# The written order of an attention stage, with another table of prices for changes of work on TensorE

## The chip, the cores and the metric

The kernel runs on one core of one Trainium2 chip. The metric is the device time of one execution in microseconds (us). The kernel before took 1474.77 us (median of three runs, 1473.16 to 1475.11).

## The reference, cut to what matters

One layer of a decoder is computed for a prompt of 1024 tokens and, beside it, for 8 sequences of 8 new tokens each with 2048 cached ones (64 rows, "the sample"). The change is in the order of the attention, which has no softmax. For each of 8 heads of 64 channels:

```
z = q k^T / 8 + bias(head)
log_1mb = log_sigmoid(-z) where key < query, else 0
after   = cumsum(log_1mb) over the keys, from the last key back, without the key itself
a       = exp(log_sigmoid(z) + after) where key < query, else 0
out     = a v
```

The prompt attends to its own 1024 keys; the sample attends to its 8 new keys and to 2048 cached ones, which are gathered page by page (128 keys) through a page table. Around it stand an input projection, a convolution group, an output projection, layer norms and a gated feed-forward part; the change leaves all of these alone.

## The kernel before, in words

The kernel runs stage after stage: the modulation and input projection, the attention stage, the output projection and layer norm with the first block of the up-projection, the up-projection, and the down-projection. In the trace of before the attention stage's first product starts on TensorE at 320.9 us from the start of the span, and the output projection has TensorE to itself from 618.2 us on.

The prompt's part of the attention is 96 steps, each one block of 126 keys against up to 256 queries of a pair of heads. A step's chain of work runs through all engines: `qk` (scores, TensorE, L1044 and L1045, and on blocks at the diagonal a mask product, L1048), `exp` and `ln` (ScalarE), `soft_c` (VectorE, L1055), `hi` (VectorE, L1083: the rounded half of a split) and `lo` (GpSimd, L1086: the rest), `tri` (TensorE, L1090: the running sum over keys as a product with a triangle of -1, once with each half), `weigh` (ScalarE: exp) and `accumulate` (TensorE, L1100: weights times values, two heads in two halves of the array's columns). Scores stand in 4 PSUM buffers, and the ScalarE output in 6 SBUF buffers.

The sample's part is 32 steps, each two pages of two sequences: `pages` (a load of four times 512 KB), `s_scores` (TensorE, L1233, in quarters of 32 columns of the array), `s_bias` (ScalarE), `s_turn` (TensorE, L1242: a transpose), `s_exp`, `s_ln` (ScalarE), `s_soft` and `s_after` (VectorE, L1055 and L1262), `s_tri` (TensorE, L1272 and L1273), `s_weigh` (ScalarE) and `s_values` (TensorE, L1289, in quarters of 32 columns). The pages have 6 buffers, three steps' worth.

So TensorE does four kinds of work here, which the texts below call by these letters:

- r: float32r products on the whole array (`qk`, `tri`);
- f: float32 products on the whole array (`s_turn`, `s_tri`, and small ones: `rms_b` L1117, `s_out` L1301, `last_values` L999);
- h: float32 on halves of the array's columns (`accumulate`);
- q: float32 on quarters of the columns (`s_scores`, `s_values`).

A float32 product stands in the trace as two MATMUL records, a float32r product as one. "Behind" is used for what TensorE does next: TensorE runs its list in order.

Nothing is ordered by hand. `attention_plan` writes down every piece of work with an engine, a cost in us, a priority (in prompt steps: `h` plus an offset for the prompt's work of step h, `at(s) = sb + s*sr` plus an offset for the sample's work of step s) and the work that it depends on. `run_plan` then plays this through: whenever an engine comes free it takes, of the work that could start first, the one with the lowest priority number; a penalty is added on TensorE where the work is of another kind than the last. What comes out is a list, and the kernel issues its instructions on all engines in exactly this order (manual schedule), while semaphores keep the data right. The numbers in `PAR` (offsets, step length, penalty) were found by a search that makes the planned time short. In the kernel before the plan knows three kinds (`TILED`: whole, halves, quarters): a change to the whole array costs 0.1 us (`m0`), one to halves or quarters 0.15 us (`m1`), a change between r and f nothing, and each change adds 3 steps (`md`) to the priority.

Eight blocks of the output projection's weights are loaded at the end of the stage through three staging buffers (`w_load`, SyncE's queue), rounded on VectorE (`w_hi`, L1211) and split on GpSimd (`w_lo`, L1214); their priority is `wo` plus the block's number. The output projection (L1349, L1479) waits for them. Its own order comes from the same `run_plan`, without the penalties and prices that are changed here.

Of the kernel before, what the change touches and what calls it, by code (L numbers as in the profile page):

```python
# [34 lines left out]
HI = "VVVVVVVV"  # L35
LO = "GGGGGGGG"
# [19 lines left out]
SV = ""  # L56
# [79 lines left out]
class Buf:  # L136
# [11 lines left out]
    def free(self, eng):  # L148
# [3 lines left out]
INF = 1e9  # L152
NSTEP = 32
NU = NPG // 2
PAR = dict(sb=10.07, sr=2.613, win=0, page=5.83, qk=-5.975, soft=-4.175, sc=-1.312, ca=-5.853, hi=-6.283,
           lo=-4.398, tri=-2.966, we=-1.97, ac=2.462, ss=-1.798, bi=3.89, tu=-2.19, ab=0.329, sp=-2.015,
           st=1.44, sw=-4.026, sv=2.858, rms=9.705, qp=-6.748, kp=-4.753, wo=85.118, ld=2, le=2, qd=2, qb=2,
           cn=1, cd=1, m0=0.1, m1=0.15, md=3)
LOW = "G" * 8


def attention_plan(par):
# [3 lines left out]
    P = par  # L166

    def add(eng, cost, prio, name, args=(), deps=(), **kw):
        W.append(Work(eng, cost, prio, name, args, deps, **kw))
        return W[-1]  # L170
# [6 lines left out]
    at = lambda s: P["sb"] + s * P["sr"]  # L177
# [24 lines left out]
    blocks = [add("DVE", 0.45, -2, "block_queries", (i,), new[0:1]) for i in range(4)]  # L202

    QK, S3, SC, CA, HI, LO, TRI, WE, AC, OUT, RG = ({} for _ in range(11))
    fre, rg, rcs = [], [], []
    for h, t in enumerate(steps):
        k = 2 * (QC - t.c0)
        z = ("z", h % 4)
        if t.first and t.j:
            prev = max(i for i in range(h) if steps[i].x == t.x)  # L210
        if t.b == max(s.b for s in steps if (s.x, s.j) == (t.x, t.j)) and t.j:
# [6 lines left out]
                 banks=(z,))  # L218
# [4 lines left out]
                    [SC[h], CA.get(h - 2), TRI.get(h - 2), HI.get(h - 1)])  # L223
        eng, cost = ("DVE", 0.068 + 0.00104 * k) if h < P["ld"] or h >= N - P["le"] else ("Pool", 0.1 + 0.0022 * k)
        LO[h] = add(eng, cost, h + P["lo"], "lo", (h,), [HI[h]])
        TRI[h] = add("PE", 0.04 + 0.00083 * k, h + P["tri"], "tri", (h,), [LO[h], HI[h]], banks=(z,))
        WE[h] = add("Activation", 0.054 + 0.00083 * k, h + P["we"], "weigh", (h,), [TRI[h]], banks=(z,))
        if t.b:

# [5 lines left out]
                    banks=(acc,))  # L235
        if t.last and t.j == 7:
            add("DVE", 0.35, h + P["rms"], "out_last", (h,), [AC[h]], banks=(acc,))
        elif t.last:
            n = len(rg)
            OUT[h] = add("DVE", 0.73, h + P["rms"], "out", (h,), [AC[h]] + ([rg[n - 2]] if n >= 2 else []), banks=(acc,))  # L240
            a = add("Activation", 0.31, h + P["rms"], "rms_a", (h,), [OUT[h]] + ([rg[n - 1]] if n else []))
            b = add("PE", 0.45, h + P["rms"], "rms_b", (h,), [a], take="sz")
            c = add("Activation", 0.36, h + P["rms"], "rms_c", (h,), [b], give=b)
# [3 lines left out]
        if t.x == 1 and h // 2 % 12 == 0 and t.p < 3:  # L247
# [8 lines left out]
            r = [d]  # L256
# [3 lines left out]
            for e in range(2):  # L260
                a = add("DVE", 0.6, pr, "k_hi", (p, e), [d])
# [4 lines left out]
            if p == 3:  # L266
                lv = add("DVE", 0.3, pr, "last_load", (), VN[3])
                for i in range(5):
                    a = add("PE", 0.25, pr, "last_values", (i,), [lv], take="sz")
                    b = add("Activation", 0.3, pr, "last_copy", (i,), [a], give=a)  # L270
# [10 lines left out]
    sn = nb  # L281
# [11 lines left out]
    PG, SS, BI, TU, A3, SP, LA, ST, SW, SV, OB, OT = ({} for _ in range(12))  # L293
    for s in range(NSTEP):
        PG[s] = add("DMA", P["page"], at(s) - 9, "pages", (s,), [SV.get(s - 3), PG.get(s - 1)])
        b = (("scr", s % 2),)
        SS[s] = add("PE", 0.86, at(s) + P["ss"], "s_scores", (s,), [PG[s], BI.get(s - 2), ST.get(s - 2), sn, SS.get(s - 1)] + blocks, banks=b)
        BI[s] = add("Activation", 0.36, at(s) + P["bi"], "s_bias", (s,), [SS[s], TU.get(s - 2)], banks=b)
        TU[s] = add("PE", 0.15, at(s) + P["tu"], "s_turn", (s,), [BI[s], SW.get(s - 2), nbv], banks=b, take=s % 2)
        a = add("Activation", 0.265, at(s) + P["ab"], "s_exp", (s,), [TU[s], SP.get(s - 2)], banks=b)  # L300
        A3[s] = add("Activation", 0.31, at(s) + P["ab"], "s_ln", (s,), [a])
        SP[s] = add("DVE", 0.335, at(s) + P["sp"], "s_soft", (s,), [A3[s], ST.get(s - 2), LA.get(s - 1)], banks=b)
        LA[s] = add("DVE", 0.7, at(s) + P["sp"], "s_after", (s,), [SP[s], LA.get(s - 1)])
        ST[s] = add("PE", 0.68, at(s) + P["st"], "s_tri", (s,), [SP[s], LA[s], TU[s]], banks=b)
        SW[s] = add("Activation", 0.265, at(s) + P["sw"], "s_weigh", (s,), [ST[s], SV.get(s - 2)], banks=b, give=TU[s])
        SV[s] = add("PE", 0.88 + (0.5 if s % NU == 0 else 0), at(s) + P["sv"], "s_values", (s,),
                    [SW[s], SV.get(s - 1), OB.get(s - 1), nbv, nbe, zero], banks=(("acc", 1),))
        if s % NU == NU - 1:
            OB[s] = add("DVE", 0.61, at(s) + P["sv"], "s_ob", (s,), [SV[s], OT.get(s - NU)], banks=(("acc", 1),))
            a = add("PE", 0.43, at(s) + P["sv"] + 1, "s_out", (s,), [OB[s]], banks=(("acc", 0),))  # L310
            OT[s] = add("DVE", 0.7, at(s) + P["sv"] + 1, "s_osT", (s,), [a], banks=(("acc", 0),))
    e = at(NSTEP) + 2
    a = add("Activation", 0.27, e, "o_a", (), [OT[NSTEP - 1]] + rg[-2:])
# [31 lines left out]
    return 2.2 if a == "DMA" else 0.28 if b == "PE" else 0.15 if (a, b) == ("Activation", "DVE") else 0.2  # L345


TILED = {"s_scores": 32, "s_values": 32, "accumulate": 64}
PORT = {"hi", "q_hi", "k_hi", "k_copy", "fix_zero", "block_queries", "rms_gain", "o_gain", "w_hi"}
HOLD = {"lo", "q_lo", "k_lo", "w_lo", "q_ones"}  # L350

# [1 line left out]
def run_plan(W, P):  # L353


    lat, win, tune = 0.2, P["win"], "sb" in P
    mode, held = [128], {"DVE": [0.0, 0.0], "Pool": [0.0, 0.0]}

    def switch(w):
        m = TILED.get(w.name, 128)  # L360
        return 0.0 if not tune or w.eng != "PE" or m == mode[0] else P["m0"] if m == 128 else P["m1"]

    def keeps(w):
        return tune and (w.eng == "DVE" and (w.name in PORT or w.name in HOLD) or w.eng == "Pool" and w.name in HOLD)
    free, bank, region, out, rings = {}, {}, {0: 0.0, 1: 0.0}, [], {k: list(v) for k, v in P.get("rings", {}).items()}
    succ, need = {}, {}
    for w in W:
        need[w] = len(w.deps)
        for d in w.deps:
            succ.setdefault(d, []).append(w)  # L370
    ready = {}
    for w in W:
        if not need[w]:
            ready.setdefault(w.eng, []).append([0.0, w])

    def start(r, w):
        s = max(r, free.get(w.eng, 0.0))
        for b in w.banks:
            e, t = bank.get(b, (None, 0.0))
            if e != w.eng:  # L380
                s = max(s, t + lat)
        if keeps(w):
            a, b = held["Pool" if w.eng == "DVE" else "DVE"]
            if a <= s < b:
                s = b
        if w.take == "sz":
            t = min(region.values())
            s = max(s, t)
        elif w.take is not None:
            s = max(s, region[w.take])  # L390
        new = {}
        for b in w.uses:
            if b.slot is None:
                l = rings.setdefault(b.ring, [])
                i = len(l) + new.get(b.ring, 0)
                new[b.ring] = new.get(b.ring, 0) + 1
                if b.before and b.before.slot is None:
                    s = INF
                if i >= b.n:
                    s = max(s, l[i - b.n].free(w.eng))  # L400
        return s

    while True:
        best = None
        for e, l in ready.items():
            if not l:
                continue
            c = [(start(r, w), w) for r, w in l]
            m = min(s for s, _ in c)
            if m >= INF:  # L410
                continue
            s, w = min(((s, w) for s, w in c if s <= m + win), key=lambda a: (a[1].prio + (P["md"] if tune and switch(a[1]) else 0), a[0]))
            if best is None or s < best[0]:
                best = (s, w)
        if best is None:
            break
        s, w = best
        w.start, w.end = s, s + w.cost + switch(w)
        if w.eng == "PE":
            mode[0] = TILED.get(w.name, 128)  # L420
        if keeps(w):
            held[w.eng] = [s, w.end]
        free[w.eng] = w.end
        ready[w.eng] = [a for a in ready[w.eng] if a[1] is not w]
        for b in w.banks:
            bank[b] = (w.eng, w.end)
        if w.take is not None:
            i = min(region, key=region.get) if w.take == "sz" else w.take
            w.region = i
            region[i] = INF  # L430
        for b in w.uses:
            if b.slot is None:
                b.slot = len(rings[b.ring])
                rings[b.ring].append(b)
        if w.give is not None:
            region[w.give.region] = w.end + (0.3 if w.name == "rms_c" else 0)
        out.append(w)
        for n in succ.get(w, ()):
            need[n] -= 1
            if not need[n]:  # L440
                r = max(d.end + latency(d.eng, n.eng) for d in n.deps)
                ready.setdefault(n.eng, []).append([r, n])
    assert len(out) == len(W), [(w.name, w.args) for w in W if w.end is None][:5]
    return out
# [1575 lines left out]
```

## Time and profile before

| | |
|---|---|
| median of three runs | 1474.77 us |
| the profiled execution | 1474.22 us |
| its span, first to last instruction | 1472.4 us |
| TensorE busy | 1410.7 us, 96% |
| VectorE, ScalarE, GpSimd busy | 74%, 41%, 39% |
| attention stage, 320.9 to 605.1 us | 284.2 us, TensorE busy 267.77 us |

Busy time of TensorE is read with care: a MATMUL record begins when the product starts to stream, while its end is modelled, so records overlap, and a wait that is shorter than a product's pipeline shows as no idle time. The distance from one start to the next is the better measure of what a piece of work occupies.

### The profile page before, as it was taken

To read this page: it belongs to the slowest core of one execution; us is meant where nothing else is said; L and a number is where in the kernel's file an instruction comes from. 1 tells how busy PE (TensorE), PEld (TensorE's weight loads), DVE (VectorE), ACT (ScalarE), POOL (GpSimd) and SP (SyncE) were. 2 spreads that over 40 slices of the span, in tenths; PEclk is the share of its full clock that TensorE was granted. 3 is DMA by queue.
4 is the path that set the end of the run, shared out by engine and by line. 5 is a ranking of instruction groups with operands and counts; after the bars stand their busy time and mean duration, and the time that the engine had idled before them with its cause. 6 is when DMAs were issued, how large, how long until landed. Compare 5 with 4: busy or idle time off the path is not lost.

```text
span 1472.4 us, 26908 instructions
## 1 busy us (share of the span) xinstructions
PE 1410.7 (96%) x10254; PEld 1228.3 (83%) x10254; DVE 1091.3 (74%) x1927; ACT 609.3 (41%) x1212; POOL 579.1 (39%) x433
## 2 busy tenths in 40 slices
PE   7999899998999999799889999999999989999997
PEld 4998789985666676488889999999999978888886
DVE  5799999447676765678788777877787754178798
ACT  2544413638898888324443333333333333031110
POOL 0397732126464543514444434443444323016200
PEclk9999999999999999899999999999999999999999
DMA  8755532258988888443222222222222256153331
GB/s 335 243 175 167 163 104 90 77 177 270 304 303 305 293 270 296 134 142 107 87 64 88 74 75 73 89 73 75 73 89 73 75 175 237 41 165 95 107 101 71
DMA packets 116988, 219.26 MB, mean 149 GB/s; under 512 B 28674, under 2 KB 71211, under 8 KB 116603
## 3 DMA queue, kind: packets, MB, share of 16 engines
q1 hardware_dynamic: 113498, 206.03, 42.8%
q0 software_dynamic: 3360, 11.51, 2.2%
q8 instruction: 81, 1.33, 0.4%
q14 instruction: 49, 0.39, 0.1%
HBM read 184.31 MB, written 32.68 MB: 147 GB/s over the span
## 4 chain that ended last, share of the span: by engine, by line
PE 64%; DVE 4%; ACT 1%; issue 1%; DMA 1%; POOL 0%; DVEq 0%; POOLq 0%; ACTq 0%
PE pu L1780 23%; PE pd L1911 18%; PE scr L1780 7%; PE pu L1479 3%; PE scr L1479 2%; PE acc L1100 2%; PE z L1090 1%; PE scr L1233 1%; PE acc L1289 1%; PE z L1044 1%; PE z L1045 1%; PE scr L1272 1%; PE scr L1273 1%; DVE Y L1592 0%; POOL wo L1214 0%
## 5 line engine op out<-in xcount | busy, mean ns | idle before, releaser
L1911 PE MATMUL pd<-wd,ft 128*128 128x512 f32 (+1 forms) x1186 | 263.3, 384 | 4.4 <-ACT ft L576 4.4
L1911 PEld LDWEIGHTS pd<-wd,ft 128*128 128x128 f32 x1186 | 218.8, 190 | 48.8 <-ACT ft L576 5.3
L1780 PE MATMUL pu<-X,wA 128*128 128x272 f32 x768 | 187.6, 288 | 0.0
L1780 PE MATMUL pu<-Y,wA 128*128 128x272 f32 x756 | 186.7, 288 | 0.0
L613 PE MATMUL po<-HH,whi 128*128 128x378 f32 (+1 forms) x464 | 153.3, 339 | 0.2 <-ACT HH L576 0.2
L613 PE MATMUL po<-HL,whi 128*128 128x378 f32 (+1 forms) x464 | 152.4, 334 | 0.5 <-DVE HL L577 0.4
L613 PE MATMUL po<-HH,wlo 128*128 128x378 f32 (+1 forms) x464 | 152.2, 334 | 0.0
L1780 PEld LDWEIGHTS pu<-X,wA 128*128 128x128 f32 x768 | 141.5, 188 | 0.0
L1086 POOL TENSOR_TENSOR ll<-l,lh 127x512 fp32r<-127x512 f32 (+4 forms) x92 | 96.4, 1048 | 114.1 <-DVE lh L1083 81.2
L1780 PEld LDWEIGHTS pu<-Y,wA 128*128 128x128 f32 x756 | 140.6, 189 | 0.0
L845 ACT ACTIVATE l<-z 127x512 f32<-127x512 f32 (+11 forms) x272 | 119.9, 475 | 33.8 <-PE z L1090 11.9
L701 DVE SCALAR_TENSOR_TENSOR pc<-u,vec,pc 128x1024 f32<-128x1024 f32 x80 | 102.6, 1282 | 1.3
L1756 POOL TENSOR_TENSOR cc__8771<-raw 128x512 f32<-128x512 f32 x20 | 33.0, 1649 | 167.7 <-DMA raw<-w_up 159.0
L613 PEld LDWEIGHTS po<-HH,whi 128*128 128x128 f32 x464 | 87.5, 190 | 8.2 <-ACT whi L576 3.3
L613 PEld LDWEIGHTS po<-HH,wlo 128*128 128x128 f32 x464 | 88.2, 191 | 4.3 <-issue 3.7
L577 DVE TENSOR_TENSOR wA<-raw,wA 128x512 fp32r<-128x512 f32 x60 | 75.8, 1264 | 20.8 <-ACT wA L576 20.6
L613 PEld LDWEIGHTS po<-HL,whi 128*128 128x128 f32 x464 | 87.6, 190 | 3.9 <-issue 1.7
L685 POOL TENSOR_TENSOR cv<-cv,q 128x1024 f32<-128x1024 f32 x36 | 88.8, 2468 | 3.1 <-ACT q L684 1.4
L1055 DVE SCALAR_TENSOR_TENSOR l<-l,z 127x512 f32<-127x512 f32 (+4 forms) x96 | 53.4, 557 | 46.6 <-ACT l L845 44.4
L576 ACT ACTIVATE wA<-raw 128x512 fp32r<-128x512 f32 x60 | 38.0, 633 | 117.9 <-PE pu L1780 66.3
L576 ACT ACTIVATE ft<-fr 128x896 fp32r<-128x896 f32 (+3 forms) x27 | 25.5, 943 | 127.0 <-PE pd L1911 121.8
L1932 POOL TENSOR_TENSOR fx<-fx,rows 128x1024 f32<-128x1024 f32 (+1 forms) x9 | 23.2, 2587 | 121.1 <-DMA fx<-xscr 121.1
(656 smaller groups left out, 3612.0 us busy)
## 6 DMA issues: line engine op xcount, KB each, us to landing
kv<-kv SPq DMA_DIRECT2D x128, 512.0 KB
catt<-w_ada SPq DMA_DIRECT2D x48, 512.0 KB
raw<-w_up SPq DMA_DIRECT2D x44, 512.0 KB
fscr<-vt SPq DMA_DIRECT2D x22, 512.0 KB
raw<-w_down SPq DMA_DIRECT2D x22, 512.0 KB
raw<-w_in SPq DMA_DIRECT2D x20, 512.0 KB
fr<-fscr SPq DMA_DIRECT2D x16, 448.0 KB
xT<-xT SPq DMA_DIRECT2D x8, 544.0 KB
```

The costliest lines, as they stand in the source:

```text
L576: A.activation(hi, x, AF.Copy)
L577: V.tensor_sub(lo, x, hi)
L613: PE.matmul(ps[c][:, 0:b - a], wt[:, 128 * kt:128 * kt + 128], xt[:, kt, a:b], start=first and kt == 0, stop=last and kt == KT - 1)
L685: G.tensor_tensor(op, op, t[:, 0:TP], op=OP.add)
L701: V.scalar_tensor_tensor(pcs[c], src, w, pcs[c], op0=OP.mult, op1=OP.add)
L845: A.activation(out, in_, f, **kw)
L1055: V.scalar_tensor_tensor(out, e, ZMAX, z, op0=OP.min, op1=OP.max)
L1086: (V if eng == "DVE" else G).tensor_tensor(t.hl[1], t.l, t.hl[0], op=OP.subtract)
L1479: PE.matmul(po[c](), xs()[:, xt, kt % 4], WO[kt][:, wt, 512 * c:512 * c + 512], start=kt == KORD[0] and (xt, wt) == passes[0], stop=kt == ...
L1756: G.tensor_tensor(s1, a21, a22, op=OP.add)
L1780: PE.matmul(p[g][:, 0:NB], W[i][wt][:, 128 * kt:128 * kt + 128], X[g][kt][xt][:, i, :], start=i < 3 and kt == 0 and n == 0, stop=kt == 3 a ...
L1911: PE.matmul(pd[c], fx[:, xt, i], w[:, wt, cw * c:cw * c + cw], start=i == 0 and (xt, wt) == passes[0], stop=i == nf - 1 and (xt, wt) == pa ...
```

## The change

The plan gets other kinds, other prices for a change of kind, another form of the penalty, three other costs, and other numbers in `PAR`. What is computed, the instructions, their number, the buffers and the code of the other stages stay the same; the order of the attention stage's list comes out anew on every engine.

The kinds are now r, f, h and q as above. A change between r and f costs 0.25 us in the plan, either way; into h 0.15; into q nothing, while `s_scores` and `s_values` themselves cost 1.0 instead of 0.86 and 0.88; from h 0.1 to r and 0.12 to f; from q 0.1 to r and 0.08 to f. `tri` costs 0.01 more. The penalty on the priority is no longer 3 steps for each change but 30 steps per us of the price: 7.5 steps between r and f, 4.5 into h, none into q, 3 back to r from h or q, 3.6 and 2.4 back to f.

Of the offsets, those that move most are (before, after): `hi` -6.283, -24.531; `sc` (`soft_c`) -1.312, -9.78; `sp` (`s_soft`, `s_after`) -2.015, 14.719; `ab` (`s_exp`, `s_ln`) 0.329, -7.005; `sw` (`s_weigh`) -4.026, -9.55; `wo` 85.118, 98.352.

```diff
-PAR = dict(sb=10.07, sr=2.613, win=0, page=5.83, qk=-5.975, soft=-4.175, sc=-1.312, ca=-5.853, hi=-6.283,
-           lo=-4.398, tri=-2.966, we=-1.97, ac=2.462, ss=-1.798, bi=3.89, tu=-2.19, ab=0.329, sp=-2.015,
-           st=1.44, sw=-4.026, sv=2.858, rms=9.705, qp=-6.748, kp=-4.753, wo=85.118, ld=2, le=2, qd=2, qb=2,
-           cn=1, cd=1, m0=0.1, m1=0.15, md=3)
+PAR = dict(sb=10.063, sr=2.628, win=0, page=5.83, qk=-4.726, soft=-4.375, sc=-9.78, ca=-6.623, hi=-24.531,
+           lo=-5.271, tri=-2.825, we=-1.466, ac=3.032, ss=-2.745, bi=5.993, tu=-3.027, ab=-7.005, sp=14.719,
+           st=0.971, sw=-9.55, sv=3.072, rms=9.339, qp=-5.002, kp=-3.097, wo=98.352, ld=2, le=2, qd=2.497, qb=2,
+           cn=1, cd=1, md=30)
...
-        TRI[h] = add("PE", 0.04 + 0.00083 * k, h + P["tri"], "tri", (h,), [LO[h], HI[h]], banks=(z,))
+        TRI[h] = add("PE", 0.05 + 0.00083 * k, h + P["tri"], "tri", (h,), [LO[h], HI[h]], banks=(z,))
...
-        SS[s] = add("PE", 0.86, at(s) + P["ss"], "s_scores", (s,), [PG[s], BI.get(s - 2), ST.get(s - 2), sn, SS.get(s - 1)] + blocks, banks=b)
+        SS[s] = add("PE", 1.0, at(s) + P["ss"], "s_scores", (s,), [PG[s], BI.get(s - 2), ST.get(s - 2), sn, SS.get(s - 1)] + blocks, banks=b)
...
-        SV[s] = add("PE", 0.88 + (0.5 if s % NU == 0 else 0), at(s) + P["sv"], "s_values", (s,),
+        SV[s] = add("PE", 1.0 + (0.5 if s % NU == 0 else 0), at(s) + P["sv"], "s_values", (s,),
...
-TILED = {"s_scores": 32, "s_values": 32, "accumulate": 64}
+
+KIND = {"qk": "r", "tri": "r", "accumulate": "h", "s_scores": "q", "s_values": "q"}
+CHANGE = {("f", "r"): 0.25, ("h", "r"): 0.1, ("q", "r"): 0.1, ("r", "f"): 0.25, ("h", "f"): 0.12, ("q", "f"): 0.08,
+          ("r", "h"): 0.15, ("f", "h"): 0.15, ("q", "h"): 0.15}
...
     def switch(w):
-        m = TILED.get(w.name, 128)
-        return 0.0 if not tune or w.eng != "PE" or m == mode[0] else P["m0"] if m == 128 else P["m1"]
+        return CHANGE.get((mode[0], KIND.get(w.name, "f")), 0.0) if tune and w.eng == "PE" else 0.0
...
-            s, w = min(((s, w) for s, w in c if s <= m + win), key=lambda a: (a[1].prio + (P["md"] if tune and switch(a[1]) else 0), a[0]))
+            s, w = min(((s, w) for s, w in c if s <= m + win), key=lambda a: (a[1].prio + (P["md"] * switch(a[1]) if tune else 0), a[0]))
...
         if w.eng == "PE":
-            mode[0] = TILED.get(w.name, 128)
+            mode[0] = KIND.get(w.name, "f")
```

## Rows read from the trace of the kernel before

**Rows 1.** The page: busy time of TensorE and ScalarE over the whole execution (busy us, share of the span, instructions), and the chain that ended last, by engine.

```profile
PE 1410.7 (96%) x10254; PEld 1228.3 (83%) x10254; DVE 1091.3 (74%) x1927; ACT 609.3 (41%) x1212; POOL 579.1 (39%) x433
...
PE 64%; DVE 4%; ACT 1%; issue 1%; DMA 1%; POOL 0%; DVEq 0%; POOLq 0%; ACTq 0%
```

**Rows 2.** Busy time of each engine in four stretches: the attention stage, the gap behind it, and the stage's middle and end. Columns: stretch, its length, busy us (instructions) of each engine, granted clock, share of the DMA engines, GB/s.

```profile
320.90:605.10 284.20, 267.77 (x2933) 182.16 (x2930) 195.23 (x483) 231.45 (x566) 148.07 (x151) 0.99 0.82 279
605.10:618.20 13.10, 8.79 (x26) 5.77 (x26) 7.26 (x12) 2.44 (x6) 10.17 (x4) 0.78 0.59 172
345.00:590.00 245.00, 238.85 (x2663) 163.16 (x2661) 167.62 (x414) 207.91 (x511) 126.43 (x132) 1.00 0.83 286
590.00:605.10 15.10, 8.62 (x74) 4.39 (x72) 13.50 (x22) 6.40 (x15) 9.07 (x4) 1.00 0.40 114
```

**Rows 3.** What TensorE waited for in the attention stage: total us, times, longest us.

```profile
PE z L1044 <- ACT l L845: 3.5, 6, 0.9
PE z L1090 <- DVE ll L1086: 2.3, 2, 2.1
PE acc L1301 <- DVE ob L1295: 1.4, 1, 1.4
```

**Rows 4.** TensorE in order of time around one `s_tri` and one `s_turn` that stand between float32r products: start us, modelled us, line, tiles, shape, count.

```profile
408.29 0.39 PE L1090 MATMUL z<-lh,negr 127*127 127x512 f32 x1
408.52 0.39 PE L1090 MATMUL z<-ll,negr 127*127 127x512 f32 x1
408.75 0.59 PE L1272 MATMUL scr<-spt,cst 128*128 128x256 f32 x2
...
409.61 0.38 PE L1242 MATMUL scr<-cst,ssc 128*128 128x128 f32 x2
409.75 0.48 PE L1090 MATMUL z<-lh,negr 127*127 127x512 f32 x1
410.06 0.40 PE L1090 MATMUL z<-ll,negr 127*127 127x512 f32 x1
```

**Rows 5.** The same view around `s_scores` and then an `s_tri`, each between float32r products.

```profile
470.77 0.40 PE L1090 MATMUL z<-ll,negr 127*127 127x512 f32 x1
471.09 1.07 PE L1233 MATMUL scr<-kv,qbd 128*32 128x256 f32 x16
472.09 0.50 PE L1090 MATMUL z<-lh,negr 127*127 127x512 f32 x1
472.43 0.40 PE L1090 MATMUL z<-ll,negr 127*127 127x512 f32 x1
472.66 0.59 PE L1272 MATMUL scr<-spt,cst 128*128 128x256 f32 x2
...
473.34 0.47 PE L1044 MATMUL z<-QS,KS 128*127 128x256 f32 x1
```

**Rows 6.** The same view: one `accumulate` between float32r products, and two `accumulate` in a row (x8).

```profile
502.49 0.40 PE L1090 MATMUL z<-ll,negr 127*127 127x512 f32 x1
502.81 0.65 PE L1100 MATMUL acc<-l,vn 127*64 127x256 f32 x4
503.39 0.28 PE L1090 MATMUL z<-lh,negr 127*127 127x16 f32 x1
...
555.37 1.08 PE L1100 MATMUL acc<-l,vn 127*64 127x256 f32 x8
556.39 0.50 PE L1090 MATMUL z<-lh,negr 127*127 127x512 f32 x1
```

**Rows 7.** The same view: `s_values` and `s_scores` in a row between float32r products.

```profile
475.99 1.08 PE L1289 MATMUL acc<-kv,sar 128*32 128x128 f32 x32
476.88 1.05 PE L1233 MATMUL scr<-kv,qbd 128*32 128x256 f32 x16
477.86 0.50 PE L1090 MATMUL z<-lh,negr 127*127 127x512 f32 x1
```

**Rows 8.** The same view: an `s_tri` between `s_scores` and `accumulate`, and an `s_turn` between `s_values` and `accumulate`.

```profile
369.33 0.70 PE L1272 MATMUL scr<-spt,cst 128*128 128x256 f32 x2
...
370.39 0.29 PE L1100 MATMUL acc<-l,vn 127*64 127x8 f32 x4
...
484.36 0.44 PE L1242 MATMUL scr<-cst,ssc 128*128 128x128 f32 x2
484.73 0.65 PE L1100 MATMUL acc<-l,vn 127*64 127x256 f32 x4
```

**Rows 9.** The first and the last of the 69 rows with L1100 in the timeline of TensorE over the stage (a row is an unbroken run of `accumulate`; there are 96 of them), and below them the first and the last of the 12 places where one of `s_scores` and `s_values` is directly followed by the other.

```profile
328.48 0.72 PE L1100 MATMUL acc<-l,vn 17*64 17x16 f32 x8
...
600.65 0.65 PE L1100 MATMUL acc<-l,vn 127*64 127x256 f32 x4 [0.69 <-ACT l L845]
...
412.08 1.08 PE L1289 MATMUL acc<-kv,sar 128*32 128x128 f32 x32
...
586.82 1.07 PE L1233 MATMUL scr<-kv,qbd 128*32 128x256 f32 x16
```

**Rows 10.** The chain that ended last, in order of time, where it passes the stage's end: start us, us, what.

```profile
606.65 3.04 POOL wo L1214
609.71 4.56 DMA raw<-w_out
...
615.67 2.47 POOL wo L1214
```

More of the change, by code (lines that the diff above doesn't have):

```diff
@@ L356, in run_plan @@
     lat, win, tune = 0.2, P["win"], "sb" in P
-    mode, held = [128], {"DVE": [0.0, 0.0], "Pool": [0.0, 0.0]}
+    mode, held = ["r"], {"DVE": [0.0, 0.0], "Pool": [0.0, 0.0]}
     def switch(w):
-        m = TILED.get(w.name, 128)
-        return 0.0 if not tune or w.eng != "PE" or m == mode[0] else P["m0"] if m == 128 else P["m1"]
+        return CHANGE.get((mode[0], KIND.get(w.name, "f")), 0.0) if tune and w.eng == "PE" else 0.0
     def keeps(w):
```

## The prediction

> **What bounds the kernel now.** I read the page first: TensorE is busy 96% of the span and carries most of the chain that ended last [rows 1]. Since the change touches the order of the attention stage alone, the stretches come next: of that stage's 284.2 us TensorE is busy 267.8, in its middle 238.85 of 245, at a granted clock of 1.00; ScalarE, next in line, reaches 207.9 there [rows 2]. The reader is to see that the stage is as long as TensorE's list takes, with two remainders: waits for ScalarE and for the split on GpSimd, short and scattered [rows 3], and an end (590 to 605.1 us) in which TensorE is busy 8.6 of 15.1 us [rows 2]. So a new order is worth what it changes in the products' own spacing and in these waits. That spacing is in the timeline of TensorE, from start to start, and I compare it with the plan's prices.
>
> **Prices, trace against plan.** Behind a float32r product, `tri` begins its second half after 408.52 - 408.29 = 0.23 us, behind float32 on the whole array after 410.06 - 409.75 = 0.31, so entering r from f costs 0.08 [rows 4]. Leaving r for f costs nothing: the last `tri` product holds its 0.23 us (408.52 to 408.75) [rows 4]. An `s_tri` between float32r products takes 473.34 - 472.66 = 0.68 us [rows 5], an `s_turn` 0.14, both together 0.86 and 0.14 [rows 4]. A visit to f with one `s_tri` thus occupies 0.68 + 0.08 = 0.76 us. The plan charged 0.68 before and charges 0.68 + 0.25 + 0.25 = 1.18 after.
>
> A visit to q: the product before it takes 0.32 instead of 0.23, `s_scores` itself 1.00, and the next `tri` 0.34 instead of 0.23 [rows 5], together 0.09 + 1.00 + 0.11 = 1.20. The plan charged 0.86 + 0.25 = 1.11 and charges 1.0 + 0.1 = 1.10. Two in a row take 477.86 - 475.99 = 1.87 [rows 7], so 2.07 with entry and exit, and joining two visits saves 2.40 - 2.07 = 0.33; in the plan it saved 0.25 and now saves 0.1.
>
> A visit to h: the product before it again takes 0.32, `accumulate` 0.58 [rows 6], and for what follows I take q's 0.11: 0.78. The plan has 0.43 + 0.25 = 0.68 both times. Two in a row take 556.39 - 555.37 = 1.02 [rows 6], 1.22 with entry and exit; joining saves 0.34, in the plan 0.25 both times.
>
> So the prices of h and q visits hardly move, and the one that does is that between r and f, which the trace shows at 0.08 a visit. What the plan will do to save it shows in rows too: an `s_tri` with q before and h behind takes 1.06 us, an `s_turn` 0.37 [rows 8], against 0.76 and 0.14 + 0.08 = 0.22 between float32r products: 0.30 and 0.15 more, where the plan believes it saves.
>
> The Trainium skill, "TensorEngine Tiling (Array Packing)", section "Key Properties", says that changing the tiling mode drains TensorE; it names no such cost for a change of data type. By that rule too r and f change for nothing, the 0.3 us in [rows 8] are the price of tiling on both sides, and a plan that counts r to f would end later; that is the first rival below.
>
> **The change part by part.**
>
> *Entering h.* The penalty rises from 3 to 4.5 steps and `ac` from 2.46 to 3.03, so against float32r work an `accumulate` waits 2 steps longer; one becomes ready each step, so it more often finds a second one beside it. Today 96 of them stand in 69 runs, 27 joined [rows 9]. Bounds: no change, and all in pairs (48 runs, 21 more joined, -7.1 us). I take half, 11: 11 x 0.34 = -3.7 us. The ScalarE output has 6 buffers, and `exp` of a later step waits for them; two steps' delay fits.
>
> *Entering q.* Its penalty falls from 3 to 0, so a ready `s_scores` is taken at once and seldom waits for an `s_values`. Of 12 joined ones [rows 9] I let 3 go: 3 x 0.33 = +1.0 us (bounds 0 to 12: +4.0; or 8 more joined, because the two are both free to enter, -2.6).
>
> *f between tiled work.* Of the 32 `s_tri` and 32 `s_turn` I let 10 each move away from float32r neighbours. With a tiled neighbour on one side alone the exit from it is paid anyway, so that place costs nothing; with one on both sides 0.30 and 0.15. A third of the latter: 10 x 0.10 + 10 x 0.05 = +1.5 us. Bounds: 0, and 20 each at the dear place, 20 x 0.45 = +9.0.
>
> *Waits.* TensorE is idle 245 - 238.85 = 6.2 us in the middle and 15.1 - 8.6 = 6.5 at the end [rows 2]. Waits come where the plan believed something ready earlier than it is. The plan's q work now lasts what the trace shows, so the loads and the sample's chain keep step with it better; I take a quarter off, -3.2 us. Bounds: half of it gone (-6.3); or half as much again (+6.3), since each r-f change that the plan still makes is charged 0.5 us for some 0.1, TensorE then arrives early, and what it finds unfinished is `lo` or `weigh`, as in [rows 3].
>
> *Other engines.* `hi` and `soft_c` go ahead of everything on VectorE, `s_soft` and `s_after` behind it; VectorE is busy 168 of 245 us [rows 2], so what is set back finds a place soon and I count nothing. If that cover fails, `s_tri`, then `s_weigh` and `s_values` are late and the page buffers come free late; SyncE's list behind that load then waits too, and the key and query loads with it. The last wait of this kind costs what the sample's end costs now, up to 6.5 us. On ScalarE `s_exp` and `s_weigh` go ahead of the prompt's `exp`; they hold that up by one instruction and shorten the sample's chain: both signs, nothing counted. The DMA share is 0.83 [rows 2]: a stage shorter by 2% leaves room.
>
> *The weights at the end.* `w_hi` and `w_lo` fall from 85 to 98 in priority, behind every `lo` on GpSimd. They run when the last `lo` are done anyway, and what bounds them is the ring of three buffers: split 3.04, load 4.56, split 2.47 us [rows 10]. Counted as nothing; bounds one load later, +4.6, and GpSimd's idle time in the gap closed, 13.1 - 10.2 = -2.9 [rows 2].
>
> **The sum.** -3.7 + 1.0 + 1.5 - 3.2 = -4.4 us on the profiled execution of 1474.22 us: 1469.8. That execution is 0.55 below the median of the runs, so the forecast is 1470.4 us.
>
> **Rivals.**
>
> *Slower: the price that isn't there.* The search pays with real changes of tiling for r-f changes that cost 0.08. For it: the rows above, and the largest penalty of all (7.5 steps) stands on just that change. With 15 `s_tri` and 15 `s_turn` between tiled work (+6.8), 6 more single q visits (+2.0), 4 more joined `accumulate` (-1.4) and waits down by 1: +6.4, 1481.2 us. It decides once the dear places outweigh the gains of the forecast: (3.7 + 3.2 - 1.0) / 0.225 = 26 of the 64 pieces. Against it: from f the way to q is free in the plan, and leaving h or q for r costs only 3 steps, so f can also end up with a tiled neighbour on one side, which costs nothing.
>
> *No change.* The order is reshuffled and the sums cancel, since visits to h and q are priced as before and the own work of TensorE is the same: 1474.5 us. For it: TensorE's list holds 96% of the stage [rows 2] whatever its order. Against it: so many priorities move that it would be chance.
>
> *Much faster.* The higher prices let the plan see TensorE as full as it is: pairs of `accumulate` nearly throughout and half of the waits gone, -7.1 - 6.3 = -13.4: 1461.4 us.
>
> **How the numbers follow.** 0.2% is about what a measurement of this kernel can tell from no change, here 3 us. The forecast with its own range (1465 to 1471.5) 0.33, much faster 0.11, slower 0.34, no change 0.22. So faster 0.44, same 0.22, slower 0.34. The range for 8 in 10 goes from 1461 (much faster) to 1484: the slower rival with two thirds of the dearest bounds (+9.0 and +4.0 would give 1487.8 with nothing gained).
>
> **What would show it.** A right forecast has the stage's stretch from 320.9 us to its last `accumulate` about 4 us shorter, about 58 rows of L1100 instead of 69, and less idle time of TensorE at the same busy time of the other engines. The slower rival shows `s_tri` of 1.06 us in place of 0.68, and more TensorE busy time in a stage with no more waits. The changes between r and f should be far fewer in either case; if these are fewer and the stage shorter by more than the tiling and the waits explain, the price of 0.25 was right and my reading of [rows 4, 5] wrong. Behind 618 us all should stand as before, shifted; a difference there would be a fault of mine.

## The result, and the profile after

The kernel after took 1483.07 us (median of four runs, 1481.21 to 1484.81), the kernel before 1474.37 us beside it: a ratio of 1.0059, 95% interval 1.0047 to 1.0072. The change made the kernel slower by some 8.7 us. The profiled execution took 1481.21 us, its span is 1479.1 us. Lines of after are those of before plus 2 (`qk` L1046, `soft_c` L1057, `tri` L1092, `accumulate` L1102).

The page's busy times of after answer to [rows 1]:

```profile
PE 1412.9 (96%) x10254; PEld 1231.9 (83%) x10254; DVE 1097.4 (74%) x1927; ACT 610.1 (41%) x1212; POOL 577.9 (39%) x433
```

The instructions are the same in number. What grew is in the stage. First the stretch from the first `qk` to the end of the last `accumulate` in the windows of before, which [rows 2] do not have, and a shorter one that is needed below (columns as there):

```profile
320.90:601.25 280.35, 267.10 (x2932) 181.89 (x2929) 192.33 (x479) 230.26 (x563) 145.22 (x150) 0.99 0.83 281
...
358.00:367.00 9.00, 8.98 (x92) 5.53 (x91) 8.71 (x19) 7.71 (x16) 7.73 (x9) 1.00 0.82 262
```

and the same stretches of after, with the middle of [rows 2] between them:

```profile
320.80:607.80 287.00, 269.03 (x2930) 184.92 (x2928) 196.87 (x480) 231.15 (x563) 146.63 (x150) 0.98 0.79 276
...
345.00:590.00 245.00, 235.50 (x2594) 161.40 (x2596) 167.95 (x405) 203.79 (x499) 123.71 (x128) 0.99 0.81 281
...
358.00:367.00 9.00, 5.81 (x49) 3.84 (x49) 8.32 (x15) 4.87 (x11) 6.46 (x6) 0.81 0.67 246
```

The stretch is 287.00 - 280.35 = 6.65 us longer, nearly all of the span's 6.7. TensorE's idle time in it went from 13.25 to 17.97 (+4.72), its busy time grew by 1.93. And 9 us from 358 on stand out: TensorE busy 5.8 instead of 9.0 and a granted clock of 0.81. What TensorE waited for in after's stretch (columns as [rows 3]):

```profile
PE z L1046 <- ACT l L847: 7.1, 5, 3.2
PE scr L1235 <- DMA kv<-kv: 2.5, 3, 1.8
PE z L1092 <- DVE ll L1088: 2.3, 2, 2.1
PE scr L1119 <- ACT sq L847: 2.0, 1, 2.0
PE acc L1102 <- DVE osT L1311: 1.9, 1, 1.9
```

Against [rows 3], `qk` waits 7.1 us for ScalarE instead of 3.5, 3.2 of them at once. The last two rows belong to the end of the sample's chain, behind 600 us. TensorE's timeline after shows the long wait:

```profile
353.73 1.08 PE L1291 MATMUL acc<-kv,sar 128*32 128x128 f32 x32
354.74 0.39 PE L1046 MATMUL z<-raw,KS 128*127 128x256 f32 x1
...
355.40 0.65 PE L1102 MATMUL acc<-l,vn 127*64 127x256 f32 x4
...
356.74 0.65 PE L1102 MATMUL acc<-l,vn 127*64 127x256 f32 x4
357.32 0.50 PE L1092 MATMUL z<-lh,negr 127*127 127x512 f32 x1
...
358.98 0.59 PE L1275 MATMUL scr<-spt,cst 128*128 128x256 f32 x2
362.76 0.49 PE L1046 MATMUL z<-raw,KS 128*127 128x256 f32 x1 [3.19 <-ACT l L847]
...
363.83 1.12 PE L1102 MATMUL acc<-l,vn 127*64 127x256 f32 x4
364.88 1.74 PE L1291 MATMUL acc<-kv,sar 128*32 128x128 f32 x32
366.56 0.50 PE L1092 MATMUL z<-lh,negr 127*127 127x512 f32 x1
```

An `accumulate` occupies 357.32 - 356.74 = 0.58 us ahead of the pause and 364.88 - 363.83 = 1.05 behind it, an `s_values` 1.01 (353.73 to 354.74) and 1.68 (364.88 to 366.56), a `qk` 0.66 (354.74 to 355.40) and 1.07 (362.76 to 363.83): after 3.19 us without work TensorE ran for a while at the lower of its two levels (1.2 instead of 2.4 GHz), which the granted clock of 0.81 says as well. Whom ScalarE waited for is in its own timeline, and whom VectorE served in VectorE's; GpSimd stands below them (after, all three):

```profile
356.11 0.63 ACT L847 ACTIVATE l<-l 127x512 f32<-127x512 f32 x1
...
361.65 1.06 ACT L847 ACTIVATE l<-z 1x512 f32<-1x512 f32 x2 [3.76 <-DVE l L1057]
...
355.03 3.44 DVE L961 CAST KH<-raw 64x1008 fp32r<-64x1008 f32 x2
358.49 1.05 DVE L969 CAST KH<-raw 64x16 fp32r<-64x16 f32 x1
359.57 1.08 DVE L970 CAST KS<-KH 64x16 fp32r<-64x16 f32 x1
360.66 0.17 DVE L971 TENSOR_TENSOR KS<-raw,KH 64x16 fp32r<-64x16 f32 x1
360.87 0.69 DVE L1057 SCALAR_TENSOR_TENSOR l<-l,z 127x512 f32<-127x512 f32 x1
...
358.01 2.61 POOL L976 TENSOR_TENSOR KS<-raw,KH 64x504 fp32r<-64x504 f32 x2
```

Read from below: while GpSimd splits keys (358.01 to 360.62), VectorE runs two copies of 64x16 elements in 1.05 and 1.08 us; the subtraction behind them, with GpSimd idle, takes 0.17. These three are the plan's `k_copy`, 0.45 us in its prices. Behind them `soft_c` starts at 360.87. Its input was ready when `ln` ended, at 356.11 + 0.63 = 356.74, so it is 4.1 us late: up to 358.47 VectorE was still at the two large key roundings (`k_hi`, L961, 3.44 us together), and the copies took the other 2.4 us. Why a later `qk` waits for this: once `soft_c` is done, ScalarE copies one row of the running sum of an earlier step into its tile (`carry`, the 1x512 of the row at 361.65; it belongs to a step's chain too) and runs that earlier step's `weigh`. Only then is the earlier step's PSUM buffer free, and the next `qk` writes into it. The same happens at 416.5 to 421.95 us, in the same views of after:

```profile
416.71 1.28 DVE L970 CAST KS<-KH 64x16 fp32r<-64x16 f32 x1
418.00 0.17 DVE L971 TENSOR_TENSOR KS<-raw,KH 64x16 fp32r<-64x16 f32 x1
418.19 1.05 DVE L969 CAST KH<-raw 64x16 fp32r<-64x16 f32 x1
419.28 1.10 DVE L970 CAST KS<-KH 64x16 fp32r<-64x16 f32 x1
...
416.68 1.28 POOL L1088 TENSOR_TENSOR ll<-l,lh 127x512 fp32r<-127x512 f32 x1 [0.37 <-DVE KH L969]
418.04 2.30 POOL L976 TENSOR_TENSOR KS<-raw,KH 64x504 fp32r<-64x504 f32 x2
...
421.95 0.38 PE L1046 MATMUL z<-QS,KS 128*127 128x256 f32 x1 [2.16 <-ACT l L847]
```

A copy ends when the GpSimd instruction beside it ends: 416.71 + 1.28 = 417.99 against 416.68 + 1.28 = 417.96, and 419.28 + 1.10 = 420.38 against 418.04 + 2.30 = 420.34. The Trainium skill, "SBUF — State Buffer", section "Who interferes with whom", says that VectorE and GpSimd share a port pair that one of them holds for a whole instruction while the other blocks fully, and counts casts among what can take it; the trace agrees to 0.04 us.

The plan knows of this, but for a piece of work as a whole (`PORT`, `HOLD` in `run_plan`): it holds `k_copy` back until the split then running is done, once, and charges 0.45 us for all three. On the chip each of the three can be caught anew by the next split. Played through by its own code, the plan of after has these two `soft_c` held up for 0.14 and 0.45 us. All six groups, summed by line (busy us and count behind the stretch): L967, L968, L969 of before,

```profile
340.00:495.00 155.00, 3.72 (x6) 1.00 0.85 286
340.00:495.00 155.00, 2.07 (x6) 1.00 0.85 286
340.00:495.00 155.00, 3.22 (x6) 1.00 0.85 286
```

and L969, L970, L971 of after:

```profile
340.00:495.00 155.00, 3.74 (x6) 0.99 0.82 285
340.00:495.00 155.00, 5.87 (x6) 0.99 0.82 285
340.00:495.00 155.00, 2.50 (x6) 0.99 0.82 285
```

9.0 us before, 12.1 after, 6 x 0.45 = 2.7 in the plan. Before was hit as well, but its `qk` waits for ScalarE no longer than 0.9 us at once [rows 3].

### The profile page after: what moved, and what is told of

Its sections match the earlier page's. It is cut to its first block, busy times and chain, and to the rows that moved or that the text cites. A ratio compares the mean times of both kernels' runs of the same rounds, so it can differ in the third digit from the quotient of the medians.

```text
span 1479.1 us, 26929 instructions
## 1 busy us (share of the span) xinstructions
PE 1412.9 (96%) x10254; PEld 1231.9 (83%) x10254; DVE 1097.4 (74%) x1927; ACT 610.1 (41%) x1212; POOL 577.9 (39%) x433
## 4 chain that ended last, share of the span: by engine, by line
PE 60%; DVE 3%; ACT 1%; DMA 1%; issue 1%; POOL 1%; SPq 0%; DVEq 0%; ACTq 0%; POOLq 0%
PE pu L1782 23%; PE pd L1913 18%; PE scr L1782 7%; PE pu L1481 3%; PE scr L1481 2%; PE z L1092 1%; PE acc L1102 1%; PE acc L1291 1%; PE scr L1235 1%; PE z L1046 1%; DVE Y L1594 0%; PE z L1047 0%; ACT l L847 0%; PE scr L1721 0%; DMA kv<-kv 0%
## 5 line engine op out<-in xcount | busy, mean ns | idle before, releaser
L847 ACT ACTIVATE l<-z 127x512 f32<-127x512 f32 (+12 forms) x272 | 118.4, 474 | 33.6 <-PE z L1092 11.0
L1758 POOL TENSOR_TENSOR cc__8771<-raw 128x512 f32<-128x512 f32 x20 | 28.9, 1444 | 167.9 <-DMA raw<-w_up 147.9
L1057 DVE SCALAR_TENSOR_TENSOR l<-l,z 127x512 f32<-127x512 f32 (+4 forms) x96 | 53.1, 556 | 48.1 <-ACT l L847 45.4
L1802 DVE SCALAR_TENSOR_TENSOR gc<-gp,vec,gc 128x1024 f32<-128x1024 f32 x42 | 71.4, 1700 | 0.0
```

What stands on the lines that cost most here:

```text
L847: A.activation(out, in_, f, **kw)
L1057: V.scalar_tensor_tensor(out, e, ZMAX, z, op0=OP.min, op1=OP.max)
L1802: V.scalar_tensor_tensor(cp_, gpk, w, cp_, op0=OP.mult, op1=OP.add)
```

## The experiments

**Three theories.** K: the small key copies ahead of a `soft_c` that is due carry the loss. P, my slower rival: the price of 0.25 us between r and f, where the trace shows 0.08 in all, makes TensorE's list worse. O: the new offsets make longer waits under any table of prices. The first set undoes one part at a time:

`e1_rf_free`, after without that price; `e2_new_par_old_prices`, before with after's offsets; `e3_old_par_new_prices`, after with before's offsets; `e4_kcopy_later`, after's list with each `k_copy` moved behind the next `soft_c`. e1:

```diff
-CHANGE = {("f", "r"): 0.25, ("h", "r"): 0.1, ("q", "r"): 0.1, ("r", "f"): 0.25, ("h", "f"): 0.12, ("q", "f"): 0.08,
+CHANGE = {("f", "r"): 0.0, ("h", "r"): 0.1, ("q", "r"): 0.1, ("r", "f"): 0.0, ("h", "f"): 0.12, ("q", "f"): 0.08,
```

e2 and e3 exchange the two `PAR` of the diff ahead of the prediction, e2 with `m0=0.1, m1=0.15, md=3` kept and e3 with `md=30`. e4:

```diff
-        for w in attention_plan(PAR):
+        plan = attention_plan(PAR)
+        for w in [w for w in plan if w.name == "k_copy"]:
+            i = plan.index(w)
+            n = next(j for j in range(i, len(plan)) if plan[j].name == "soft_c")
+            first = min(j for j in range(len(plan)) if w in plan[j].deps)
+            if n < first:
+                plan.insert(n, plan.pop(i))
+        for w in plan:
```

> The changed kernel with one edit: a change between float32 and float32r costs nothing in the plan (price and penalty 0 both ways), all else as in the changed kernel. Theory P (the price that isn't there makes the order worse): it falls back to the kernel before or below, 1470 to 1476 us. Theory O (the new offsets and penalties make an order whose waits are longer, whatever the table): it stays at 1480 to 1485 us. Theory K (the small copies of the key preparation stand on VectorE just ahead of the work that TensorE needs next): it falls only as far as the new order happens to move these copies, and the idle time of TensorE tells.

> The kernel before with the changed kernel's offsets, but the old prices of changes, the old flat penalty of 3 steps and the old costs. Theory P: 1470 to 1476 us, as before, since the price is gone. Theory O: 1479 to 1485 us. Theory K: near the changed kernel where the copies come as early (their offset kp is the new one), 1478 to 1484 us.

> The changed kernel with the offsets of the kernel before and the new prices and penalties. Theory P: 1480 to 1490 us, slower than before, with more TensorE time for changes of tiling. Theory O: 1472 to 1477 us, as before. Theory K: as before, since the offset of the copies is the old one, unless the list moves them.

> The changed kernel with its list kept, but each of the six groups of small key copies is issued behind the next softplus of a prompt step on VectorE instead of ahead of it. Theory K: TensorE's idle time of 3.2 us near 359 us and of 2.2 us near 420 us gets shorter, the clock doesn't fall near 363 us, and the time falls by 3 to 6 us, to 1477 to 1480. Theories P and O: no change beyond 1 us, 1482 to 1484, since TensorE's list is the same.

Measured, each against before on the same chip: e1 1.0074 (1.0057 to 1.0091), e2 1.0119 (1.0087 to 1.0152), e3 1.0088 (1.0064 to 1.0111), e4 1.0019 (1.0005 to 1.0032). Neither half of the change alone does better than both.

- e1: with after's offsets, taking the price away gains nothing, as O foretold and P did not.
- e2, with the same offsets, is slower than any theory had it. In its trace two groups of copies in a row, 4.7 us from 358.28 to 362.98, hold up a `soft_c`, and `qk` waits 3.6 us.
- e3 came out where P put it, against O and K. In its trace 8 `s_tri` and 12 `s_turn` stand between tiled work on both sides, where before has 3 and 3: at 0.30 and 0.15 us these are some 2.9 us, a part of its loss. So P is out as the cause of after's loss, but with before's offsets the new prices do bring about what P says.

A caution on e1 to e3: offsets were found for one table of prices and are used with another, which is a handicap of its own.

e4 decides for K: moving eighteen small instructions, with TensorE's list untouched, takes 0.40 of the 0.59% away, 5.9 us at the upper edge of K's 3 to 6, where P and O allow 1. `qk`'s waits for ScalarE in e4, against 7.1, 5, 3.2 in after, and TensorE's timeline of e4 where after had 3.19 us:

```profile
PE z L1046 <- ACT l L847: 1.4, 3, 0.8
...
359.88 0.39 PE L1046 MATMUL z<-raw,KS 128*127 128x256 f32 x1 [0.84 <-ACT l L847]
```

The wait is 3.19 - 0.84 = 2.35 us shorter, and the copies had taken 2.38 ahead of `soft_c` (358.49 to 360.87). The 0.84 that stay are likely due to the two large roundings: e4 keeps them where they were, and its `soft_c` starts right behind them. e4's VectorE there, `soft_c` first and the copies behind it, one of them again long:

```profile
357.98 0.69 DVE L1057 SCALAR_TENSOR_TENSOR l<-l,z 127x512 f32<-127x512 f32 x1
358.58 0.42 DVE L969 CAST KH<-raw 64x16 fp32r<-64x16 f32 x1
359.04 1.09 DVE L970 CAST KS<-KH 64x16 fp32r<-64x16 f32 x1
```

The window of e4 from 358 to 367 us has its clock back:

```profile
358.00:367.00 9.00, 7.86 (x81) 4.42 (x79) 7.93 (x16) 7.07 (x16) 7.24 (x7) 1.00 0.93 325
```

**Another way to the same end, and before with the same edits.** `e5_kcopy_pool` is after, `e7_before_pool` before, `e8_rf_free_pool` e1 with the copies on GpSimd; `e6_before_later` is before with the edit of e4.

```diff
-        V.tensor_copy(KH[R, e, 8, 1:17], kf[R, 1008:TP])
-        V.tensor_copy(KS[R, e, 8, 1:17], KH[R, e, 8, 1:17])
-        V.tensor_sub(KS[O, e, 8, 1:17], kf[R, 1008:TP], KH[R, e, 8, 1:17])
+        G.tensor_copy(KH[R, e, 8, 1:17], kf[R, 1008:TP])
+        G.tensor_copy(KS[R, e, 8, 1:17], KH[R, e, 8, 1:17])
+        G.tensor_tensor(KS[O, e, 8, 1:17], kf[R, 1008:TP], KH[R, e, 8, 1:17], op=OP.subtract)
```

> The changed kernel, list kept, with the small key copies (three per group, six groups, 64 partitions x 16 elements) issued on GpSimd instead of VectorE at the same place of the list. Theory K (VectorE is held up by these copies while GpSimd runs a long instruction beside them): softplus and the rounding of the prompt's steps start up to 4 us earlier near 361 and 420 us, TensorE's idle time there goes, time falls by 4 to 8 us against the changed kernel, to within 3 us of the kernel before. Rival Q (it was only the place in VectorE's list, and the copies now hold up GpSimd's split in the same way): 0 to 3 us.

> The kernel before with the edit of the second of my runs on these copies: each group behind the next softplus. Theory K: its waits near 429 and 488 us (0.7 and 1.1 us by the trace) shrink, 1 to 2 us faster than before. Rival S (the list of before was found among many and has its copies where they do no harm): within 1 us of before, or up to 3 us slower.

> The kernel before with the small key copies on GpSimd. Theory K: 1 to 2 us faster than before. Rival S: within 1 us of before.

> The kernel of the first run (changed kernel, no price between float32 and float32r) with the small key copies on GpSimd. Theory K: 3 to 6 us faster than without, about 1477 to 1480 against a before of 1472. Rival S: its waits are elsewhere (4.8 us behind the sample's triangle product near 433 us), so at most 2 us faster.

Measured: e5 1.0016 (1.0004 to 1.0028), e6 1.0025 (1.0015 to 1.0036), e7 1.0012 (0.9999 to 1.0025), e8 1.0045 (1.003 to 1.0059). Two independent ways of freeing `soft_c` give after nearly the same 6 us back (5.9 and 6.3), and e8 is 0.29% faster than e1, 4.3 us, as K foretold (3 to 6). For before K foretold 1 to 2 us less, and that failed: e6 is 0.25% slower and e7 0.12% (its interval just reaches before), nearer to rival S. Their waits say why; e7, then e6:

```profile
PE z L1090 <- POOL ll L1086: 2.1, 3, 0.7
PE z L1044 <- ACT l L845: 1.3, 3, 0.8
...
PE scr L1272 <- DVE spt L1055: 2.4, 2, 1.7
PE z L1044 <- ACT l L845: 1.3, 3, 0.8
```

`qk`'s wait for ScalarE does shrink in both, from the 3.5 us of [rows 3], but others grow in its place: in e7 `tri` waits 2.1 us for the split on GpSimd, which now runs the copies too (before has no such wait), in e6 `s_tri` waits 2.4 instead of 0.7. So neither edit is free, and the copies are worth moving where a long wait hangs on them, as in after; before's list had no such place. e8 against e5 says once more that with after's offsets the price between r and f is not what hurts. What e4 and e5 still lack to before (0.16 to 0.19%) has its likeliest places in the page loads and at the sample's end: in e5 TensorE waits 3.2 us for pages and 2.0 for `sq`, where before waited 0.7 for pages and, at the sample's end, 1.4 for `ob` (the last of [rows 3]); this was not tried by itself. What else makes e6 slower than before is open.

**Offsets found anew.** For a fair test of the price, new offsets were looked for under three tables: before's, after's, and after's with 0 between r and f. Each candidate list was played through with the distances from start to start that the traces show, and with splits on GpSimd and roundings on VectorE excluding each other one instruction at a time; the one that ended first was kept. In `r1` to `r7` only `PAR` differs (and the price, as in e1, where the name says rf_free). `r1_before_prices`:

```diff
-PAR = dict(sb=10.07, sr=2.613, win=0, page=5.83, qk=-5.975, soft=-4.175, sc=-1.312, ca=-5.853, hi=-6.283,
-           lo=-4.398, tri=-2.966, we=-1.97, ac=2.462, ss=-1.798, bi=3.89, tu=-2.19, ab=0.329, sp=-2.015,
-           st=1.44, sw=-4.026, sv=2.858, rms=9.705, qp=-6.748, kp=-4.753, wo=85.118, ld=2, le=2, qd=2, qb=2,
-           cn=1, cd=1, m0=0.1, m1=0.15, md=3)
+PAR = dict(sb=9.777, sr=2.676, win=0, page=5.83, qk=-12.901, soft=-8.832, sc=-4.364, ca=-20.087, hi=-5.458,
+           lo=-18.439, tri=-12.907, we=-0.916, ac=-2.382, ss=1.039, bi=6.234, tu=-8.877, ab=-9.301, sp=-3.192,
+           st=-11.058, sw=-6.335, sv=5.871, rms=11.093, qp=-8.532, kp=-0.447, wo=140.552, ld=2, le=2, qd=7.715,
+           qb=2, cn=1, cd=1, m0=0.1, m1=0.15, md=47.48)
```

> The plan of before with its own prices and costs; only the numbers in PAR are new. They come from a search in which each candidate list is played through with the distances from start to start that the traces show for TensorE's work, with the three small copies on VectorE as separate instructions, and with split instructions on GpSimd and rounding on VectorE excluding each other; the list with the earliest end is kept. Theory K (the waits that no plan prices decide): what the plan prices does not matter once the list is chosen by the trace's distances, so this one beats before, some 0.998 (1470 to 1473 us). Theory S (before's list was favoured by chance or by selection on the chip, and a list that only looks good off the chip loses): 1.003 to 1.008, as e1 to e3.

> The plan of after with all its prices (0.25 us between r and f among them); PAR alone is found anew as for r1_before_prices. Theory K: close to before, 0.998 to 1.001, 8 us or more below after, with VectorE's small copies short or out of the way. Theory P (the price between r and f itself spoils the list, whatever the offsets): 4 us or more above the two companions, 1.003 or more. Theory S: 1.003 to 1.008, no better than its companions.

> The plan of after with the price between r and f at 0 as in e1_rf_free, and PAR found anew in the same way: the fair form of e1, which had kept offsets that were found for another price. Theory P: the fastest of the three by 4 us or more, 0.996. Theory K: within 2 us of r1_before_prices, some 0.998, since the price is paid nowhere on TensorE and only its waits count. Theory S: 1.003 to 1.008.

> The prices of after, PAR found anew as for r2_after_prices, starting from the offsets of r3_rf_free. Theory P2 (with the price of 0.25 us between r and f a plan finds worse lists, through their waits and not through TensorE's own spacing): again 1.002 or more, as r2_after_prices. Theory L (the offsets that a search happens to end on decide, and r2 was an unlucky one): anywhere from 0.998 to 1.004, mixed with r6_rf_free and r7_rf_free.

> The prices of after, PAR found anew, starting from the offsets of before. P2: 1.002 or more. L: anywhere from 0.998 to 1.004.

> The price between r and f at 0, PAR found anew as for r3_rf_free, starting from the offsets of r2_after_prices. P2: 1.000 or less, 4 us or more below r4 and r5. L: anywhere from 0.998 to 1.004.

> The price between r and f at 0, PAR found anew, starting from the offsets of before. P2: 1.000 or less. L: anywhere from 0.998 to 1.004.

Measured, with TensorE's idle time in the window from 345 to 590 us (245 less the busy time, as in [rows 2]), and the visits to h and q and changes between r and f counted in its timeline, from the first `qk` to the last `accumulate`. Idle time and counts are of one profiled execution each; r1's took 1474.07 us, where its twelve runs go from 1467.23 to 1477.47.

| | ratio (95%) | idle, us | h | q | r-f |
|---|---|---|---|---|---|
| before | 1 | 6.2 | 69 | 52 | 78 |
| after | 1.0059 (1.0047 to 1.0072) | 9.5 | 62 | 58 | 52 |
| r1, prices of before | 0.9981 (0.9968 to 0.9995) | 7.2 | 62 | 45 | 105 |
| r2, prices of after | 1.0031 (1.0018 to 1.0044) | 11.5 | 61 | 58 | 69 |
| r4, prices of after | 1.0047 (1.0028 to 1.0065) | 9.0 | 64 | 59 | 68 |
| r5, prices of after | 1.0026 (1.0013 to 1.004) | 7.1 | 65 | 60 | 74 |
| r3, r-f at 0 | 0.9988 (0.9977 to 0.9999) | 5.3 | 62 | 62 | 105 |
| r6, r-f at 0 | 0.9992 (0.9978 to 1.0007) | 7.7 | 68 | 58 | 96 |
| r7, r-f at 0 | 1.0031 (1.0019 to 1.0043) | 11.5 | 71 | 55 | 88 |

r1 (1469.52 us beside 1473.37) is faster than both kernels, if by 0.2% only, with the old prices; r3 all but equals it. The theory that before's list was merely favoured foretold 1.003 to 1.008 for all three, and falls with r1 and r3. K foretold 0.998 to 1.001 for r2 and missed it; r2 came where P put it, above its two companions by more than 4 us. On the price, five of six lists stand where P2 put them (the three with it at 1.0026 to 1.0047, two of the three without at 0.999), the sixth, r7, does not. With three on each side that is a leaning and no proof. What the table does show is that the changes of kind do not rank the lists (r2 has fewer visits to h than any and is slow), while the two with most idle time are slow under either price. Idle time in this window does not rank them all either: r4 is the slowest of the seven with 9.0 us, and r7 waits two more times for 3.0 us at the stage's end, outside it. In r2 the copies were at it again, though its search had priced them one by one; its VectorE,

```profile
482.95 1.03 DVE L969 CAST KH<-raw 64x16 fp32r<-64x16 f32 x1
484.01 1.19 DVE L970 CAST KS<-KH 64x16 fp32r<-64x16 f32 x1
485.21 1.12 DVE L971 TENSOR_TENSOR KS<-raw,KH 64x16 fp32r<-64x16 f32 x1
...
487.56 0.17 DVE L969 CAST KH<-raw 64x16 fp32r<-64x16 f32 x1
...
488.15 0.69 DVE L1057 SCALAR_TENSOR_TENSOR l<-l,z 127x512 f32<-127x512 f32 x1
```

and its TensorE:

```profile
489.51 0.38 PE L1046 MATMUL z<-QS,KS 128*127 128x256 f32 x1 [2.74 <-ACT l L847]
```

**The copies taken out of r2 and r1**, with the diff of e5:

> r2_after_prices with the small key copies on GpSimd. In r2 TensorE waits 2.74 us for ScalarE at 489.51, where VectorE ran three of the copies in 1.03, 1.19 and 1.12 us ahead of a soft_c. Theory K (the copies carry what the price table seems to cost): 1.000 to 1.0015, that wait gone. Theory P2 (the price between r and f leads to worse lists in other ways): 1.002 or more, within 1.5 us of r2.

> r1_before_prices, the fastest list so far, with the small key copies on GpSimd. Theory K with its limit (only copies that stand ahead of a soft_c that is due cost anything): r1 was chosen with the copies' collisions counted, so nothing to gain, 0.998 to 1.000. If the copies cost wherever they stand: 0.996 or less.

Measured: s1 1.0015 (1.0005 to 1.0025), against r2's 1.0031; s2 1.0001 (0.999 to 1.0011), no faster than r1. In s1 no `qk` waits there any more; the same `qk` in TensorE's timeline:

```profile
486.22 0.47 PE L1046 MATMUL z<-QS,KS 128*127 128x256 f32 x1
```

Half of what r2 loses to before thus goes with the copies, by the medians, which is the upper edge of what K foretold and more than P2 allows (2.9 us below r2, not 1.5); the two intervals overlap, so it is not clear of noise. Here too GpSimd pays: a `tri` of s1 waits 2.6 us at once for its split, where r2's longest such wait was 0.9. s2 came out just above K's range: a list without such a place gains nothing, and may lose what the copies cost GpSimd. What the lists under after's prices lose beyond the copies stays open; no single cause was isolated.

## Why the prediction was wrong

The forecast was 1470.4 us, faster; it came out slower, at 1483.07, just inside the upper end of the range (1484).

*Entering h.* 7 more `accumulate` joined (69 to 62 visits), not 11: 7 x 0.34 = -2.4 us instead of -3.7.

*Entering q.* 6 joined visits went (52 to 58 visits), not 3: +2.0 instead of +1.0. The direction of both was right.

*f between tiled work.* 4 `s_tri` and 4 `s_turn` after, 3 and 3 before: at most 0.30 + 0.15 = +0.45, instead of +1.5. The plan did save changes between r and f (78 to 52), but it put the float32 pieces at places with a tiled neighbour on one side, where the exit is paid anyway: the reason that I gave against the slower rival.

So TensorE's list comes to -2.4 + 2.0 + 0.45, about nothing by the same prices, against -1.2 foretold. This part was nearly right.

*Waits, the step that failed.* I took "a quarter off, -3.2 us", since the prices of q fit better. The stretch grew by 6.65, so waits and what followed from them cost about 6.6 us where the term said -3.2: idle time +4.72 us, and 0.47 + 0.67 + 0.41 = 1.55 us of the grown busy time for the `accumulate`, the `s_values` and the `qk` that ran at the lower clock (1.05 against 0.58, 1.68 against 1.01, 1.07 against 0.66). The rest was not assigned. That the prices of q now fit the trace gave nothing back: the waits for pages rose from 0.7 to 2.5 us. My dearer bound was +6.3, with `lo` or `weigh` found unfinished; what was unfinished was `soft_c`, behind copies that the prediction did not mention. I priced the waits as one sum that follows the quality of the prices. They follow single places: two waits of `qk`, 3.2 + 2.2 us, where its longest in [rows 3] is 0.9. Moving the copies alone gave 5.9 of the 8.7 us back (e4), so this step is shown; what the other 2.8 us are is open.

*Other engines.* "`hi` and `soft_c` go ahead of everything on VectorE", and the term of nothing that followed from it, was wrong too. A priority decides only among work that is ready when the engine comes free; at 358 us `k_copy` came first though `sc` had gone down to -9.78. VectorE was busy 168 of 245 us in both kernels, so its share told nothing of this.

*The slower rival* had the sign and nearly the time (1481.2 us), for another reason: hardly any `s_tri` and `s_turn` moved to dear places. That the range held the result is luck in the same way: its upper end was this rival's. With before's offsets (e3) the mechanism of this rival does show, and it could still act through the waits, which the lists r2 to r7 leave open.

*The rest.* Nothing behind the stage was hurt: the last `accumulate` starts 6.6 us later (600.65 to 607.24), the span ends 6.7 later. The weights at the end were counted as nothing: TensorE's waits for them in the output projection are 0.23 + 1.92 + 1.98 us before and 0.22 + 1.59 + 2.09 after.

## What to carry to other kernels

When a written order is made anew, the bound engine's list was the easy part here; the risk is in small instructions on the helpers, which cost what they may have to wait for, one by one, and not their own length. Price each instruction of a group with the lock it can meet, or move it behind the work that is due, and look at the trace again: r2's search had priced each copy, and r2 met the wait all the same. Compare two orders by the longest single waits of the bound engine, not by the planned time alone, and look for what sat on the engine two steps before the wait. That found the cause in after; it is not shown that it would rank the lists r1 to r7.

## What the runs showed of the hardware

- A cast of 64x16 elements on VectorE takes 0.17 us, and up to 1.28 us while GpSimd runs a split beside it, ending within 0.04 us of it; the subtraction is caught as well (1.12 us in r2). Larger roundings are stretched too: two of them took 3.44 us at 355.03, beside GpSimd's splits, and one at 414.49 that began ahead of the split took 0.69 (there the split took 1.68 us, where the one at 416.68 took 1.28):

```profile
414.49 0.69 DVE L961 CAST KH<-raw 64x1008 fp32r<-64x1008 f32 x1
```

- A pause of 3.19 us on TensorE was followed by a granted clock of 0.81 over 358 to 367 us, where before and e4, with no pause or one of 0.84, had 1.00.
